# Moving the turns of the S5 tables from ScalarE to VectorE, scans with a constant factor, and more buffers

## The chip, the cores and the metric

The kernel runs on one core of a Trainium2 chip. Its engines are named as in the profile: PE is TensorE (PEld its weight loads), DVE is VectorE, ACT is ScalarE, POOL is GpSimd, SP is SyncE. Each engine works through its own queue in order; engines wait for one another through semaphores. The metric is the device time in microseconds (us), lower is better. The time before is 2409.3 us, the median of three runs (2407.95 to 2409.64).

## The reference

One inference step of a two-layer backbone over 2048 latent tokens and 128 context tokens. The even layer has a gated linear attention branch and an S5 branch, the odd layer attention and a short convolution. Only the S5 branch is touched. It is a diagonal complex recurrence, run forward and backward over 32 groups of 16 channels with 64 complex states each:

```
bu_re = einsum('blgh,gph->blgp', u, bb_re);  bu_im = einsum('blgh,gph->blgp', u, bb_im)
h_t   = lb * h_(t-1) + bu_t            # complex, lb = exp(lam * dt), per state
h_re  = hf_re + flip(hb_re);  h_im = hf_im + flip(hb_im)
y5    = einsum('blgp,ghp->blgh', h_re, c_re) - einsum('blgp,ghp->blgh', h_im, c_im)
z     = gelu(y5 + s5_d * u)
```

The final states of the 128 context tokens are outputs too.

## The kernel before

The program is written with a tile framework that gives out buffers from pools and sets the order of each engine's queue by a timing model of its own, so the order below is that of the built program and not that of the Python lines. Everything is fp32; a large matmul is done as three passes over a high and a low part (`mm3`, lines 100 to 102).

Stages follow each other: input projection to u, v and gates (up to about 275 us); then the S5 core, woven with a dense projection (`qz_pass`, accumulated in the two `psD` banks and evicted by ACT into `fo`, lines 811 to 815); then GLA, GLU, the output projection and the odd layer.

The S5 core (`s5_core`) treats the 16 tokens of a chunk at once, so that a recurrence over 136 chunks (128 latent, 8 context) is left. The complex factor over a chunk is split into a magnitude, `s5_m16`, and a unit rotation. Tables C and S hold the powers of the rotation: column n of a table is the rotation by n. With them the complex recurrence becomes a real one on rotated values. One group goes through three steps:

- `first(g)`: the Toeplitz block `tz` by DMA; every second group the tables of two groups (`tables`, called when g is even); the gate tile `rgo` (line 675), which is the magnitude times a mask of ones that has a zero where the latent and the context sequence meet; and the input weights `e` on POOL.
- `second(g)`: PE transposes u into one of the three tiles `s5U` and e into `winc`, both evicted by ACT; PE multiplies them (line 708, into psW). DVE rotates the product (lines 714 to 717), runs two scans of 138 columns, one for each direction (line 722), and rotates back to H (`rh`, lines 723 to 726).
- `third(g)`: PE adds four products into psW (lines 735 to 738), ACT takes the gelu into `zy` (line 740) and stores it by two DMAs from its own queue, and copies the two final states out of H (line 731).

`weights(g + 5)` on POOL (lines 583 to 585) prepares the output weights `ct`, seven buffers, which line 738 reads last.

A table is built by doubling. ACT copies the first 16 columns, column 128 and the 9 columns of the context from small tables (lines 626 to 628). Then for m = 16, 32 and 64 the m first columns are turned by m: ACT multiplies both parts by the sine (line 637, into `tabw`), and DVE adds or subtracts the part times the cosine (line 641). For two groups and two directions that is 12 instructions on ACT and 24 on DVE, and each m needs the columns of the one before. The tables of two groups have two buffers.

A quad is four groups. The program takes 8 of the dense pass's blocks (24 matmuls each) for every quad.

Of the kernel before, what the change touches and what calls it, by code (L numbers as in the profile page):

```python
# [14 lines left out]
F32 = mybir.dt.float32  # L15
# [4 lines left out]
AF = mybir.ActivationFunctionType  # L20
OP = mybir.AluOpType
# [27 lines left out]
class Kernel:  # L49
# [317 lines left out]
    def s5_setup(self, es):  # L367
# [10 lines left out]
        self.s5_BB = c.tile([128, 2, 64, 17], F32, name="s5B")  # L378
        self.s5_A = [self.s5_AA[:, j] for j in range(2)]
        self.s5_B = [self.s5_BB[:, j] for j in range(2)]  # L380

        self.s5_go = c.tile([128, 2, 138], F32, name="s5go")
        nc.gpsimd.memset(self.s5_go, 1.0)
        nc.gpsimd.memset(self.s5_go[:, 0, 129:130], 0.0)
        nc.gpsimd.memset(self.s5_go[:, 1, 128:129], 0.0)
        self.s5_m16 = c.tile([128, 64], F32, name="s5m16")
        self.s5_h0 = self.load(c, "s5h0", a["s5h0"])
        self.s5_fin = c.tile([128, 2, 32], F32, name="s5fin")
# [1 line left out]
        self.s5_dc = self.load(c, "dcol", a["dcol"])  # L390
        sg = self.load(c, "sgn", a["sgn"])
        self.s5_U = []
        for j in range(3):
            u = c.tile([128, 2, 139], F32, name=f"s5U{j}")
            for z in (0, 129, 138):
                nc.gpsimd.memset(u[:, :, z : z + 1], 0.0)
            self.s5_U.append(u)
# [167 lines left out]
    def s5_core(self, es):  # L565
# [50 lines left out]
        def tables(g0):  # L616

            t = p.tile([128, 2, 2, 2, 138], F32, name="tabs", tag="tabs", bufs=2)
            AA, BB = self.s5_AA, self.s5_BB
            for d in range(2):  # L620
                dg = slice(d * 32 + g0, d * 32 + g0 + 2)

                at = (lambda m, n: slice(m, m + n)) if d == 0 else (lambda m, n: slice(129 - m - n, 129 - m))
                rev = (lambda n: slice(0, n)) if d == 0 else (lambda n: slice(n - 1, None, -1))
                e = 128 if d == 0 else 0
                nc.scalar.copy(t[:, :, d, :, at(0, 16)], BB[:, :, dg, rev(16)].rearrange("p c g n -> p g c n"))
                nc.scalar.copy(t[:, :, d, :, e], AA[:, :, dg, 8].rearrange("p c g -> p g c"))
                nc.scalar.copy(t[:, :, d, :, 129:138], BB[:, :, dg, rev(9)].rearrange("p c g n -> p g c n"))
            four = [(d, gg) for d in range(2) for gg in range(2)]
            for m in (16, 32, 64):  # L630

                turn = lambda j, d, gg: AA[:, j, d * 32 + g0 + gg, m // 16 : m // 16 + 1]
                at = lambda d, a: slice(a, a + m) if d == 0 else slice(129 - m - a, 129 - a)
                ws = []
                for d, gg in four:
                    ws.append(p.tile([128, 2, 64], F32, name="tabw", tag="tabw", bufs=6)[:, :, 0:m])
                    nc.scalar.activation(ws[-1], t[:, gg, d, :, at(d, 0)], AF.Copy, scale=turn(1, d, gg))  # L637
                for (d, gg), w in zip(four, ws):
                    for j, op in ((0, OP.subtract), (1, OP.add)):
                        x = t[:, gg, d, j]  # L640
                        V.scalar_tensor_tensor(x[:, at(d, m)], x[:, at(d, 0)], turn(0, d, gg), w[:, 1 - j], op0=OP.mult, op1=op)  # L641
            return t

        uv = self.u_d[0:NLAT, :].rearrange("(c t) f -> c t f", t=16)
        up = self.u_d[NLAT:NT, :].rearrange("(c t) (g h) -> c g t h", t=16, h=16)
        quad, tabs, es, tzs, Hs, gos = {}, {}, {}, {}, {}, {}

        def first(g):

            q = g // 4  # L650
            if g % 4 == 0:
                uc = p.tile([128, 16, 64], F32, name="uc", tag="uc", bufs=1)
                nc.sync.dma_start(uc, uv[:, :, 64 * q : 64 * q + 64])
                ugp = p.tile([32, 16, 16], F32, name="ugp", tag="ugp", bufs=1)
                for j in range(4):
                    nc.sync.dma_start(ugp[8 * j : 8 * j + 8], up[:, 4 * q + j])
                ug = p.tile([128, 4, 16, 16], F32, name="ug", tag="ug", bufs=2)
                nc.scalar.copy(ug, uc.rearrange("c t (g h) -> c g t h", g=4))

                pt = self.bank("T", (128, 2, 32))  # L660
                for kt in range(2):
                    nc.tensor.transpose(pt[:, kt], ugp[:, 8 * kt : 8 * kt + 8, :], self.ident[0:32, 0:32])
                ut = p.tile([128, 2, 32], F32, name="ugt", tag="ugt", bufs=2)
                nc.scalar.copy(ut, pt)
                quad[q] = ug, ut
            tz = tzs[g] = p.tile([128, 2, 256], F32, name="tz", tag="tz", bufs=2)
            src = self.f_d[g]
            for kt in range(2):
                sa = bass.AP(tensor=src.tensor, offset=src.offset + kt * 128, ap=[[16, 8], [496, 16], [1, 256]])
                nc.sync.dma_start(tz[:, kt, :], sa)  # L670
            if g % 2 == 0:
                tabs[g // 2] = tables(g)
            go = gos[g] = p.tile([128, 2, 138], F32, name="rgo", tag="rgo", bufs=3)
            for d in range(2):
                nc.scalar.activation(go[:, d], self.s5_go[:, d], AF.Copy, scale=self.s5_m16[:, d * 32 + g : d * 32 + g + 1])
            e = es[g] = pw_.tile([128, 2, 16, 16], F32, name="e", tag="e", bufs=2)
            for d in range(2):
                dg = d * 32 + g
                t1 = pw_.tile([128, 16, 16], F32, name="e1", tag="ct1", bufs=2)
                fl = (lambda v: v[:, dg, 15::-1]) if d == 0 else (lambda v: v[:, dg, 0:16])  # L680
                pw = lambda v: fl(v).unsqueeze(2).to_broadcast([128, 16, 16])
                xv = lambda v: v[:, d, g, :].unsqueeze(1).to_broadcast([128, 16, 16])
                G.tensor_tensor(t1, pw(M), xv(self.s5_Y), op=OP.mult)
                G.tensor_tensor(e[:, d], pw(R), xv(self.s5_X), op=OP.mult)
                G.tensor_tensor(e[:, d], e[:, d], t1, op=OP.add)

        def second(g):

            ug, ut = quad[g // 4]
            U = self.s5_U[g % 3]  # L690
            pt = self.bank("T", (128, 2, 128))
            for kt in range(2):
                v = slice(8 * kt, 8 * kt + 8)
# [13 lines left out]
                for kt in range(2):  # L707
                    nc.tensor.matmul(pi[:, d, :], w[:, d, kt, :], U[:, kt, d : d + 138], start=kt == 0, stop=kt == 1)
            C, S = (tabs[g // 2][:, g % 2, :, j] for j in range(2))
            go = gos.pop(g)  # L710
            A_ = p.tile([128, 2, 138], F32, name="ra", tag="ra", bufs=2)
            B_ = p.tile([128, 2, 138], F32, name="rb", tag="rb", bufs=2)
            H = Hs[g] = p.tile([128, 2, 138], F32, name="rh", tag="rh", bufs=2)
# [4 lines left out]
            af = A_.rearrange("p d c -> p (d c)")  # L718
            V.tensor_copy(af[:, 0:267:266], self.s5_h0[:, :, g])
            for d in range(2):  # L720
                sl = slice(0, 138) if d == 0 else slice(137, None, -1)
                V.tensor_tensor_scan(B_[:, d, sl], go[:, d, sl], A_[:, d, sl], 0.0, op0=OP.mult, op1=OP.add)
            V.tensor_tensor(H, B_, C, op=OP.mult)
            V.tensor_tensor(A_[0:64], B_[64:128], S[64:128], op=OP.mult)
            V.tensor_tensor(A_[64:128], B_[0:64], S[0:64], op=OP.mult)
# [1 line left out]

        def third(g):

            U, H, tz, ct = self.s5_U[g % 3], Hs.pop(g), tzs.pop(g), cts.pop(g)  # L730
            nc.scalar.copy(self.s5_fin[:, :, g], H.rearrange("p d c -> p (d c)")[:, 137:268:130])
            py = self.bank("W", (128, 2, 137))
            for kt in range(2):
                o, cs, t0 = py[:, kt], slice(128 * kt, 128 * kt + 128), 8 * kt
                nc.tensor.matmul(o, tz[:, 0, cs], U[:, 0, 1:138], start=True, stop=False)
                nc.tensor.matmul(o, tz[:, 1, cs], U[:, 1, 1:138], start=False, stop=False)
                nc.tensor.matmul(o, ct[:, 0, t0 : t0 + 8, :], H[:, 0, 0:137], start=False, stop=False)
                nc.tensor.matmul(o, ct[:, 1, t0 + 1 : t0 + 9, :], H[:, 1, 1:138], start=False, stop=True)
            zy = late.tile([128, 2, 137], F32, name="zy", tag="zy", bufs=2)
            nc.scalar.activation(zy, py, AF.Gelu_apprx_tanh)  # L740
            for kt in range(2):
                nc.scalar.dma_start(self.z_d[8 * kt : 8 * kt + 8, 16 * g : 16 * g + 16, :], zy[:, kt])

# [66 lines left out]

    def fm_store(self, dst, pc, b, ps, scale=1.0):
        nc = self.nc
        t = self.fo.tile([128, 272], F32, name="fo", tag="fo", bufs=3)
        nc.scalar.activation(t, ps, AF.Copy, scale=scale)  # L814
        nc.scalar.dma_start(dst[b * 128 : (b + 1) * 128, pc * 272 : (pc + 1) * 272], t)

# [10 lines left out]
    def zg_pass(self, hp, blocks):  # L827

        nc = self.nc

        def use(b, pc, ps):
            t = self.fo.tile([128, 272], F32, name="fo", tag="fo", bufs=3)
            nc.scalar.activation(t, ps, AF.Tanh, scale=0.5)
            nc.vector.scalar_tensor_tensor(t, t, 1.0, ps, op0=OP.add, op1=OP.mult)
            nc.gpsimd.dma_start(self.zg_d[b * 128 : (b + 1) * 128, pc * 272 : (pc + 1) * 272], t)

        return self.fm_pass(hp, blocks, use, self.h_d)
# [961 lines left out]
```

## Time and profile before

| What | Value |
|---|---|
| median of three runs | 2409.3 us |
| the profiled execution | 2415.59 us |
| its span, first to last instruction | 2413.7 us |
| mean granted TensorE clock | 0.966 |
| PE, DVE, ACT, POOL busy share of the span | 94%, 69%, 43%, 36% |

The profile is one execution, recorded engine by engine. Its own time is 1.9 us above its span and 6.3 us above the median of the timed runs. "Busy" is the time an engine spends in instructions, "idle before" the time it stood still before them, with the instruction that ended the wait. A busy DVE instruction may hold time in which it waits for memory, so a mean duration is to be compared with the shortest of the same shape.

### The profile page before, as it was taken

How to read it: one execution, taken by the hardware profiler on the slowest of the kernel's cores; microseconds unless marked ns; L12 is line 12 of the kernel's file. 1: busy time of each engine (PE TensorE's matmuls, PEld its weight loads, DVE VectorE, ACT ScalarE, POOL GpSimd, SP SyncE). 2: the span in 40 equal slices, each digit the busy share in tenths (PEclk: the TensorE clock that was granted, in tenths of full speed). 3: DMA queues.
4: the chain of work that ended last, by engine and by line, in shares of the span. 5: the costliest groups of instructions: out<-in, count | busy, mean ns of one | idle time of the engine just before them, and what ended most of it. 6: DMA issues, size and time to landing. Idle time of an engine off the chain costs nothing.

```text
span 2413.7 us, 47276 instructions
## 1 busy us (share of the span) xinstructions
PE 2268.3 (94%) x17473; PEld 2108.3 (87%) x17473; DVE 1659.3 (69%) x3916; ACT 1042.7 (43%) x2533; POOL 867.6 (36%) x1348
## 2 busy tenths in 40 slices
PE   7999887888899987999999999999999997999998
PEld 4988787887897876888888999999999997999998
DVE  4997688888866776888887665565344336676765
ACT  3554644343544453455454432233122115565653
POOL 4127165566522227767674021111101102222221
PEclk9999988999999995999999999999999998999999
DMA  9765853343469873333333642245133223222221
GB/s 322 236 210 181 252 162 99 102 132 110 131 212 310 291 232 100 123 119 123 116 115 102 210 120 80 80 138 147 50 93 102 68 69 100 88 89 88 90 69 58
DMA packets 328040, 332.90 MB, mean 138 GB/s; under 512 B 43969, under 2 KB 274977, under 8 KB 327809
## 3 DMA queue, kind: packets, MB, share of 16 engines
q1 hardware_dynamic: 265312, 238.84, 33.1%
q0 software_dynamic: 14384, 48.65, 5.9%
q10 hardware_dynamic: 48112, 42.38, 5.4%
q8 instruction: 138, 2.26, 0.4%
q14 instruction: 94, 0.76, 0.1%
HBM read 223.57 MB, written 106.22 MB: 137 GB/s over the span
## 4 chain that ended last, share of the span: by engine, by line
PE 57%; DVE 8%; issue 4%; DMA 4%; ACT 2%; POOL 2%; SPq 0%; ACTq 0%; POOLq 0%; DVEq 0%
PE psD L100 7%; PE psW L100 7%; PE psW L101 7%; PE psW L102 7%; PE psD L102 7%; PE psD L101 7%; PE psP L1081 3%; PE psW L1510 2%; PE psW L1463 2%; DVE tabs L641 2%; PE psT L1498 2%; PE psP L1098 1%; PE psP L1096 1%; DMA wst<-in_w_in_o_dram 1%; DMA wst<-h_d 1%
## 5 line engine op out<-in xcount | busy, mean ns | idle before, releaser
L100 PE MATMUL psD<-slot,yT 128*128 128x256 f32 x1088 | 318.2, 293 | 1.9 <-ACT yT L1125 1.9
L102 PE MATMUL psD<-slot,yT 128*128 128x256 f32 x1088 | 314.1, 292 | 0.0
L101 PE MATMUL psD<-slot,yT 128*128 128x256 f32 x1088 | 310.7, 286 | 0.0
L101 PE MATMUL psW<-hq,slot 128*128 128x272 f32 x1024 | 293.0, 287 | 0.0
L102 PE MATMUL psW<-hq,slot 128*128 128x272 f32 x1024 | 292.9, 287 | 0.0
L100 PE MATMUL psW<-hq,slot 128*128 128x272 f32 x1024 | 289.1, 287 | 0.0
L100 PE MATMUL psD<-hq,slot 128*128 128x272 f32 x768 | 235.1, 308 | 46.8 <-ACT fo L814 45.8
L101 PE MATMUL psD<-hq,slot 128*128 128x272 f32 x768 | 230.0, 300 | 0.0
L102 PE MATMUL psD<-hq,slot 128*128 128x272 f32 x768 | 229.5, 300 | 0.0
L100 PEld LDWEIGHTS psD<-slot,yT 128*128 128x128 f32 x1088 | 208.1, 191 | 10.0 <-ACT yT L1125 2.0
L102 PEld LDWEIGHTS psD<-slot,yT 128*128 128x128 f32 x1088 | 205.8, 191 | 4.5 <-issue 2.2
L101 PEld LDWEIGHTS psD<-slot,yT 128*128 128x128 f32 x1088 | 208.1, 191 | 1.8
L100 PEld LDWEIGHTS psD<-hq,slot 128*128 128x128 f32 x768 | 151.8, 199 | 55.2 <-ACT fo L814 48.8
L102 PEld LDWEIGHTS psW<-hq,slot 128*128 128x128 f32 x1024 | 193.1, 189 | 0.0
L101 PEld LDWEIGHTS psW<-hq,slot 128*128 128x128 f32 x1024 | 192.5, 188 | 0.0
L100 PEld LDWEIGHTS psW<-hq,slot 128*128 128x128 f32 x1024 | 190.6, 188 | 0.0
L641 DVE SCALAR_TENSOR_TENSOR tabs<-tabs,s5A,tabw 128x16 f32<-128x16 f32 (+2 forms) x384 | 146.8, 447 | 24.9 <-ACT tabw L637 23.5
L101 PEld LDWEIGHTS psD<-hq,slot 128*128 128x128 f32 x768 | 152.1, 198 | 6.4 <-issue 4.7
L102 PEld LDWEIGHTS psD<-hq,slot 128*128 128x128 f32 x768 | 152.1, 198 | 1.0 <-issue 1.0
L1472 DVE CUSTOM_DVE_ANT_0 sc<-psW,amask,sink 128x512 f32<-128x512 f32 (+1 forms) x128 | 93.6, 732 | 84.7 <-PE psT L1498 76.2
L1007 ACT ACTIVATE arg<-arg 128x512 f32<-128x512 f32 x119 | 75.0, 631 | 143.6 <-POOL arg L1006 140.3
L1475 ACT ACTIVATE sc<-sc,nm 128x512 f32<-128x512 f32 (+1 forms) x128 | 90.9, 710 | 87.9 <-DVE nm L1474 74.8
(376 smaller groups left out, 6543.2 us busy)
## 6 DMA issues: line engine op xcount, KB each, us to landing
wst<-h_d SPq DMA_DIRECT2D x96, 272.0 KB
hq<-hl_d SPq DMA_DIRECT2D x40, 544.0 KB
hl_d<-ht POOLq DMA_DIRECT2D x17, 1024.0 KB, 6.7
wada<-in_w_ada_dram SPq DMA_DIRECT2D x32, 512.0 KB
h_d<-hf SPq DMA_DIRECT2D x17, 512.0 KB
x_d<-x ACTq DMA_DIRECT2D x17, 512.0 KB
h_d<-hf ACTq DMA_DIRECT2D x17, 512.0 KB
wst<-h_d SPq DMA_DIRECT2D x34, 256.0 KB
```

Source lines behind the costliest of these rows:

```text
L100: mm(out, lh, rh, start=start, stop=False)
L101: mm(out, lh, rl, start=False, stop=False)
L102: mm(out, ll, rh, start=False, stop=stop)
L641: V.scalar_tensor_tensor(x[:, at(d, m)], x[:, at(d, 0)], turn(0, d, gg), w[:, 1 - j], op0=OP.mult, op1=op)
L1007: nc.scalar.activation(arg, arg, AF.Exp, scale=0.0625)
L1081: nc.tensor.matmul(pv[:, hh, pr, :], ak[o : o + 64, pr, :], aq[o : o + 64, pr, :], start=True, stop=True)
L1096: nc.tensor.matmul(ot, qh[o : o + 64, 0, pr, :], sf[o : o + 64, pr], start=True, stop=False)
L1463: nc.tensor.matmul(out, r32(qs[:, j, h]), kk, start=j == 0, stop=j == 1)
L1472: V.tensor_tensor_reduce(sv, ps, mask, 1.0, sk[:, h : h + 1], op0=OP.add, op1=OP.max, accum_out=m)
L1475: nc.scalar.activation(sv, src, AF.Exp, bias=nm[:, h : h + 1], accum_out=sm[:, h : h + 1])
L1498: nc.tensor.transpose(pt[:, c, :], t[:, 128 * c : 128 * c + 128], self.ident)
L1510: nc.tensor.matmul(po[kv][:, j % 2], r32(VV[:, b, kv]), r32(t[:, x, :, c, :]), start=c + x == 0, stop=c + x == nb)
```

## The change

The turns by the sine move from ACT to DVE (line 637), so a table's doubling needs no other engine after ACT's first copies. The gate tile and its mask go: a scan takes the magnitude as a constant, one column read again and again, and is split at the border of latent and context, so there are 128 and the scans have 129 and 9 columns in place of 64 of 138. There are four `s5U` tiles in place of three. The copy of the final states is written behind the gelu and kept there by the framework's `keep_in_program_order`. `zy` has three buffers in place of two and `fo` four in place of three.

```
-        self.s5_go = c.tile([128, 2, 138], F32, name="s5go")
-        nc.gpsimd.memset(self.s5_go, 1.0)
...
-        for j in range(3):
+        for j in range(4):
             u = c.tile([128, 2, 139], F32, name=f"s5U{j}")
...
                     ws.append(p.tile([128, 2, 64], F32, name="tabw", tag="tabw", bufs=6)[:, :, 0:m])
-                    nc.scalar.activation(ws[-1], t[:, gg, d, :, at(d, 0)], AF.Copy, scale=turn(1, d, gg))
+                    V.tensor_scalar(ws[-1], t[:, gg, d, :, at(d, 0)], turn(1, d, gg), None, op0=OP.mult)
...
-            go = gos[g] = p.tile([128, 2, 138], F32, name="rgo", tag="rgo", bufs=3)
-            for d in range(2):
-                nc.scalar.activation(go[:, d], self.s5_go[:, d], AF.Copy, scale=self.s5_m16[:, d * 32 + g : d * 32 + g + 1])
...
             for d in range(2):
-                sl = slice(0, 138) if d == 0 else slice(137, None, -1)
-                V.tensor_tensor_scan(B_[:, d, sl], go[:, d, sl], A_[:, d, sl], 0.0, op0=OP.mult, op1=OP.add)
+                m = self.s5_m16[:, d * 32 + g : d * 32 + g + 1]
+                for lo, n in ((0, 129), (129, 9)):
+                    sl = slice(lo, lo + n) if d == 0 else slice(lo + n - 1, lo - 1 if lo else None, -1)
+                    V.tensor_tensor_scan(B_[:, d, sl], m.to_broadcast([128, n]), A_[:, d, sl], 0.0, op0=OP.mult, op1=OP.add)
...
-            nc.scalar.copy(self.s5_fin[:, :, g], H.rearrange("p d c -> p (d c)")[:, 137:268:130])
...
-            zy = late.tile([128, 2, 137], F32, name="zy", tag="zy", bufs=2)
+            zy = late.tile([128, 2, 137], F32, name="zy", tag="zy", bufs=3)
             nc.scalar.activation(zy, py, AF.Gelu_apprx_tanh)
+            self.tc.keep_in_program_order(nc.scalar.copy(self.s5_fin[:, :, g], H.rearrange("p d c -> p (d c)")[:, 137:268:130]))
...
-        t = self.fo.tile([128, 272], F32, name="fo", tag="fo", bufs=3)
+        t = self.fo.tile([128, 272], F32, name="fo", tag="fo", bufs=4)
```

DVE's queue at the tables that stand around an even group, before (`tabs` are the tables, `psW` the product of line 708, `rb` the scanned values):

```order
L641 SCALAR_TENSOR_TENSOR tabs<-tabs,s5A,tabw 128x32 x4
L714 TENSOR_TENSOR ra<-tabs,psW 128x276
L715 TENSOR_TENSOR rb<-tabs,psW 64x276
L716 TENSOR_TENSOR rb<-tabs,psW 64x276
L641 SCALAR_TENSOR_TENSOR tabs<-tabs,s5A,tabw 128x32 x4
L641 SCALAR_TENSOR_TENSOR tabs<-tabs,s5A,tabw 128x64 x4
L717 TENSOR_TENSOR ra<-ra,rb 128x276
L641 SCALAR_TENSOR_TENSOR tabs<-tabs,s5A,tabw 128x64 x4
L719 COPY ra<-s5h_1897 128x2
L722 SCALAR_TENSOR_TENSOR rb<-rgo,ra 128x138 x2
```

The same place in the changed program, whose line numbers are some lines lower (L632 is the turn that was L637, L636 was L641, L705 to L708 were L714 to L717, L715 is the scan):

```order
L636 SCALAR_TENSOR_TENSOR tabs<-tabs,s5A,tabw 128x32 x8
L632 TENSOR_SCALAR tabw<-tabs,s5A 128x128
L705 TENSOR_TENSOR ra<-tabs,psW 128x276
L706 TENSOR_TENSOR rb<-tabs,psW 64x276
L707 TENSOR_TENSOR rb<-tabs,psW 64x276
L632 TENSOR_SCALAR tabw<-tabs,s5A 128x128 x3
L636 SCALAR_TENSOR_TENSOR tabs<-tabs,s5A,tabw 128x64 x2
L708 TENSOR_TENSOR ra<-ra,rb 128x276
L636 SCALAR_TENSOR_TENSOR tabs<-tabs,s5A,tabw 128x64 x6
L710 COPY ra<-s5h_1893 128x2
L715 SCALAR_TENSOR_TENSOR rb<-s5m_1892,ra 128x9 x2
L715 SCALAR_TENSOR_TENSOR rb<-s5m_1892,ra 128x129 x2
```

The turns now stand among the additions that read them, and each scan has become two; the group's own instructions keep their places.

ACT's queue where the tables of the next pair begin, before:

```order
L626 COPY tabs<-s5B 128x2x2x16
L731 COPY s5fin<-rh 128x2
L627 COPY tabs<-s5A 128x2x2
L815 DMA zs_d<-fo 128x272
L704 COPY winc<-psT 128x512
L628 COPY tabs<-s5B 128x2x2x9
L637 ACTIVATE tabw<-tabs,s5A 128x2x16 x2
L675 ACTIVATE rgo<-s5go,s5m_1896 128x138
```

And in the changed program (L621 to L623 are the first copies of the tables, L732 the gelu, L807 the eviction of the dense pass, L687 and L696 those of `s5U` and `winc`):

```order
L732 ACTIVATE zy<-psW 128x274
L733 COPY s5fin<-rh 128x2
L735 DMA z_d<-zy 8x16x137 x2
L807 ACTIVATE fo<-psD 128x272
L621 COPY tabs<-s5B 128x2x2x16
L622 COPY tabs<-s5A 128x2x2
L623 COPY tabs<-s5B 128x2x2x9
L808 DMA zs_d<-fo 128x272
L687 COPY s5U_1910<-psT 128x2x128
L696 COPY winc<-psT 128x512
```

The turns and gate tiles are gone from between the evictions, the final states follow the gelu at once, and the tables' first copies still stand ahead of the evictions of `s5U` and `winc`.

## Rows read from the trace of the kernel before

**Rows 1.** The page, busy time and share of each engine over the span.

```profile
PE 2268.3 (94%) x17473; PEld 2108.3 (87%) x17473; DVE 1659.3 (69%) x3916; ACT 1042.7 (43%) x2533; POOL 867.6 (36%) x1348
```

**Rows 2.** Busy time by stretch: three quads and the core's end; columns named first.

```profile
core 0: us, PE busy (x) PEld busy (x) DVE busy (x) ACT busy (x) POOL busy (x), PEclk, DMA share, GB/s
416.00:467.80 51.80, 43.68 (x330) 41.36 (x330) 42.58 (x95) 21.59 (x76) 32.90 (x49) 0.93 0.38 110
467.80:519.80 52.00, 43.41 (x330) 41.10 (x330) 42.76 (x95) 21.71 (x76) 32.98 (x50) 0.93 0.37 110
519.80:572.90 53.10, 44.58 (x330) 42.25 (x330) 42.51 (x95) 21.71 (x76) 32.82 (x49) 0.90 0.36 107
670.50:705.00 34.50, 33.40 (x271) 32.79 (x270) 24.18 (x56) 11.52 (x32) 3.95 (x6) 1.00 0.55 175
```

**Rows 3.** Waits of DVE, 285 to 700 us: total us, times, longest.

```profile
DVE ra L714 <- PE psW L708: 32.1, 11, 4.8
DVE tabs L641 <- ACT tabw L637: 23.5, 15, 2.1
```

**Rows 4.** Waits of ACT in the same stretch.

```profile
ACT tabw L637 <- DVE tabs L641: 59.8, 67, 4.0
ACT s5fin L731 <- DVE rh L726: 41.3, 28, 4.3
ACT rgo L675 <- DVE rb L722: 25.7, 12, 5.1
```

**Rows 5.** Waits of PE in the same stretch.

```profile
PE psD L100 <- ACT fo L814: 45.8, 13, 5.6
```

**Rows 6.** Groups on DVE, 285 to 700 us: busy us, mean ns | idle before.

```profile
L641 DVE SCALAR_TENSOR_TENSOR tabs<-tabs,s5A,tabw 128x16 f32<-128x16 f32 x128 | 58.6, 524 | 24.4 <-ACT tabw L637 23.5 <-issue 0.9
L641 DVE SCALAR_TENSOR_TENSOR tabs<-tabs,s5A,tabw 128x64 f32<-128x64 f32 x128 | 45.4, 414 | 0.2
L641 DVE SCALAR_TENSOR_TENSOR tabs<-tabs,s5A,tabw 128x32 f32<-128x32 f32 x128 | 44.7, 402 | 0.3
L722 DVE TENSOR_TENSOR_SCAN rb<-rgo,ra 128x138 f32<-128x138 f32 x64 | 35.0, 587 | 1.0
L724 DVE TENSOR_TENSOR ra<-rb,tabs 64x276 f32<-64x276 f32 x32 | 19.9, 623 | 0.4
L725 DVE TENSOR_TENSOR ra<-rb,tabs 64x276 f32<-64x276 f32 x32 | 19.5, 608 | 0.4
L726 DVE TENSOR_TENSOR rh<-rh,ra 128x276 f32<-128x276 f32 x32 | 19.1, 597 | 1.0
L723 DVE TENSOR_TENSOR rh<-rb,tabs 128x276 f32<-128x276 f32 x32 | 18.3, 572 | 1.0
```

**Rows 7.** DVE in order of time, 515 to 575 us: start, us, instructions.

```profile
523.84 0.86 DVE L641 SCALAR_TENSOR_TENSOR tabs<-tabs,s5A,tabw 128x64 f32<-128x64 f32 x4
524.63 0.15 DVE L719 COPY ra<-s5h 128x2 f32<-128x2 f32 x1
524.81 0.78 DVE L722 TENSOR_TENSOR_SCAN rb<-rgo,ra 128x138 f32<-128x138 f32 x2
526.09 0.44 DVE L724 TENSOR_TENSOR ra<-rb,tabs 64x276 f32<-64x276 f32 x1
544.44 4.64 DVE L641 SCALAR_TENSOR_TENSOR tabs<-tabs,s5A,tabw 128x64 f32<-128x64 f32 x8
```

**Rows 8.** POOL in order of time, 515 to 575 us.

```profile
547.13 1.26 POOL L583 TENSOR_TENSOR ct<-s5M,s5CY 128x272 f32<-128x272 f32 x2
559.15 1.40 POOL L584 TENSOR_TENSOR ct<-s5R,s5CX 128x272 f32<-128x272 f32 x2 [9.57 <-PE psW L738]
```

**Rows 9.** POOL's groups, 285 to 700 us: first and last of six.

```profile
L685 POOL TENSOR_TENSOR e<-e,e 128x256 f32<-128x256 f32 x60 | 43.9, 752 | 0.0
L583 POOL TENSOR_TENSOR ct<-s5M,s5CY 128x272 f32<-128x272 f32 x50 | 31.5, 651 | 0.0
```

**Rows 10.** A DVE multiplication by a column, in the setup, 100 to 300 us.

```profile
L416 DVE TENSOR_SCALAR s5M<-q,sgn 128x64 f32<-128x64 f32 x1 | 0.3, 279 | 0.0
```

More of the change, by code (lines that the diff above doesn't have):

```diff
@@ L380, in s5_setup @@
         self.s5_B = [self.s5_BB[:, j] for j in range(2)]
-        self.s5_go = c.tile([128, 2, 138], F32, name="s5go")
-        nc.gpsimd.memset(self.s5_go, 1.0)
-        nc.gpsimd.memset(self.s5_go[:, 0, 129:130], 0.0)
-        nc.gpsimd.memset(self.s5_go[:, 1, 128:129], 0.0)
         self.s5_m16 = c.tile([128, 64], F32, name="s5m16")
@@ L645, in s5_core @@
         up = self.u_d[NLAT:NT, :].rearrange("(c t) (g h) -> c g t h", t=16, h=16)
-        quad, tabs, es, tzs, Hs, gos = {}, {}, {}, {}, {}, {}
+        quad, tabs, es, tzs, Hs = {}, {}, {}, {}, {}
         def first(g):
@@ L689, in second @@
             ug, ut = quad[g // 4]
-            U = self.s5_U[g % 3]
+            U = self.s5_U[g % 4]
             pt = self.bank("T", (128, 2, 128))
@@ L709, in second @@
             C, S = (tabs[g // 2][:, g % 2, :, j] for j in range(2))
-            go = gos.pop(g)
             A_ = p.tile([128, 2, 138], F32, name="ra", tag="ra", bufs=2)
@@ L728, in third @@
         def third(g):
-            U, H, tz, ct = self.s5_U[g % 3], Hs.pop(g), tzs.pop(g), cts.pop(g)
-            nc.scalar.copy(self.s5_fin[:, :, g], H.rearrange("p d c -> p (d c)")[:, 137:268:130])
+            U, H, tz, ct = self.s5_U[g % 4], Hs.pop(g), tzs.pop(g), cts.pop(g)
             py = self.bank("W", (128, 2, 137))
@@ L831, in use @@
         def use(b, pc, ps):
-            t = self.fo.tile([128, 272], F32, name="fo", tag="fo", bufs=3)
+            t = self.fo.tile([128, 272], F32, name="fo", tag="fo", bufs=4)
             nc.scalar.activation(t, ps, AF.Tanh, scale=0.5)
```

## The prediction

> **What bounds the kernel now.** I read the busy shares first. PE is busy 94% of the span [rows 1], so a change can help only where PE stands still. The stretches show one such place, and it is the one that the change touches: in the S5 core a quad of groups takes about 52 us, PE is busy 43 to 45 us of it at a granted clock of 0.90 to 0.93, and DVE 42.5 to 42.8 us [rows 2]. Both have 8 to 10 us to spare in every quad, so neither is the bound by itself: they wait for each other. After 670 us PE is busy 33.4 of 34.5 us at full clock, so there DVE has slack and PE sets the pace [rows 2].
>
> The waits tell how. PE stands 45.8 us before a dense matmul because ACT has not yet evicted `fo` [rows 5]. ACT is late because its queue is held by things that need DVE: 59.8 us before a turn whose columns DVE has not added yet, 41.3 us before the copy of the final states, 25.7 us before a gate tile whose buffer the scan still reads [rows 4]. PE's lateness comes back to DVE, which waits 32.1 us for the product of line 708, and 23.5 us for a turn [rows 3]. That is 55.6 us of waiting on DVE in a stretch of 415 us. The rest of DVE's time is work, and one more thing has to be seen in it: the same instruction has two prices. Four additions of 64 columns take 0.86 us at 523.84, eight of them 4.64 us at 544.44, which is 0.215 and 0.58 each [rows 7]. At the first POOL is idle (its next instructions stand behind waits such as the 9.57 us before 559.15), at the second it runs without a break, two instructions in 1.26 us [rows 8]. So while POOL runs, DVE gets about one instruction in for each of POOL's, whatever its length, and a hit costs 0.58 - 0.215 = 0.365 us.
>
> How many hits there are: the additions are busy 58.6 + 45.4 + 44.7 = 148.7 us, where 384 at 0.215 are 82.6, an excess of 66 us; the scans 35.0 where 64 at 0.39 (0.78 for two) are 25.0, an excess of 10; the four rotations of lines 723 to 726 76.8 where 128 at 0.44 are 56.3, an excess of 20 [rows 6, 7]. Together 96 us, or 265 hits. POOL has 328 instructions in the stretch (six groups of 50 to 60 [rows 9]), so some 63 of them hit nothing today: they fall on DVE's waits or on instructions that read psW.
>
> **The change part by part.** *The waits.* With no turn and no gate tile on ACT, and the final states copied behind a gelu whose input has needed H anyway, nothing in ACT's queue waits for DVE any more but the tables' first copies. The evictions of `fo`, `s5U` and `winc` come when PE has produced them, a fourth `s5U`, a third `zy` and a fourth `fo` keep them from waiting for a buffer, and PE can bring the next product of line 708 before DVE wants it: after a group's H, PE needs a quarter of a quad's 43 us, about 11, to the next product, and DVE has a whole group or a table in hand. So I take the 55.6 us as gone, bounds 44 to 55.6. What stays is the hand-over at the tables' first copies, which stand in ACT's queue behind a gelu and wait for line 725; they run beside line 726, so I leave 3 us of the 23.5 (bounds 0 and half, 11.8). PE's 45.8 us are not counted again: PE will stand as long, now before line 737, waiting for H, because DVE is then what is late.
>
> *The turns.* DVE gets 192 of them. The trace of before has none on DVE in this place. From below, no DVE instruction is shorter than the 0.15 us of the two-column copy [rows 7]: 28.8 us. From above by itself, a multiplication by a column took 0.279 us [rows 10]: 53.6 us. The nearest row is the addition in the same table, which also reads the table with a column as its factor, at 0.215: 41.3 us, and that I take. ACT loses the work, but ACT is busy only 22 of 52 us in a quad [rows 2], so that alone is worth nothing.
>
> *The scans.* Each becomes one of 129 columns, shorter by 9/138 of 0.39 = 0.025 us, and one of 9, at the least 0.15 us. 64 times 0.125 is 8 us; if as many of the short ones meet POOL as additions do today (66/0.365 = 181 of 384, 47%), it is 8 + 64 x 0.47 x 0.365 = 19.
>
> *POOL.* The turns put 12 more instructions into each of 16 table runs, just where POOL works. Since POOL lets one through for each of its own, the new hits are bounded by the 63 of its instructions that hit nothing today: 0 to 23 us. I take half, 12, because the turns and not the psW readers now fill POOL's stretches, while waits of DVE beside an idle POOL become work beside an idle POOL. The Trainium skill, "SBUF — State Buffer", section "SBUF: two separate sides", says that DVE and GpSimd share a port pair as an exclusive lock, held for a whole instruction, and that a DVE instruction of one source in a two-port mode takes it as one with two inputs does; by that rule a turn is hit like an addition, which is the first rival's case. The doubling of the additions' price agrees with it; a full exclusion the trace does not show, for the 42.8 us of DVE and 33.0 of POOL stand in one quad of 52.
>
> *The end.* After 670 us one pair's turns (12 at 0.215) and four groups' short scans (8 at 0.125) lie beside a PE that is the bound: 3.6 us that cost nothing. The buffers of `zy` and `fo`, and the fourth `s5U`, add no instruction but three small memsets on POOL, where the three of the mask go. Later stages have the same instructions.
>
> *Sum.* -55.6 + 3 + 41.3 + 8 + 12 - 3.6 = +5.1 us. On the profiled execution (span 2413.7 us, with 1.9 us around it 2415.6) that is 2420.7; against the median of 2409.3, which lies 6.3 us lower, it is 2414.4 us, and I say 2414. All bounds at once: -55.6 + 28.8 + 8 - 3.6 = -22 and -44 + 11.8 + 53.6 + 19 + 23 = +63 us.
>
> **The rivals.**
> *The turns meet POOL (slower).* Place: the table runs, between line 726 of an odd group and line 714 of the next. If turns and short scans are hit in 47% of the cases, as the additions are, that is 192 x 0.47 x 0.365 = 33 us and 11 more, in place of 12: 2446. For it: twelve additions in a row at the present are all hit where a POOL stretch covers a table's start. Against it: 265 + 90 + 30 hits are more than POOL's 328 instructions. With all 328 hit it is +11 over my sum, 2425. I give it 2435. It decides from my 33 hits on: each further one is loss that can be told.
> *The hand-over stays (slower).* The tables' first copies stand in ACT's queue ahead of the evictions of `s5U` and `winc`. If ACT reaches them early, those evictions wait for line 725, PE gets its product late, and half of the 32.1 us stays: 2430. For it: the order in ACT's queue. Against it: the product is wanted only after the table run.
> *DVE has room (faster).* If turns pass at 0.15 us, one behind another, and POOL's stretches move with PE's earlier line 738 so that no more is hit, it is -55.6 + 3 + 28.8 + 8 - 3.6 = -19.4 us: 2390. For it: the waits of rows 3 are real and all have their cause in ACT. Against it: DVE then works 50 of 52 us in a quad, and any lateness of PE comes on top.
>
> **How the numbers follow.** My own case (2405 to 2424 us, about even) 42%; turns meet POOL 20%; hand-over stays 8%; DVE has room 30%. A measurement of this kernel can tell about 0.2%, or 4.8 us, from no change. Faster by more: the last rival and a little of my own case, 33%. Within: 24%, the lower half of my case. Slower: its upper part, 15%, and the two slower rivals, 43% together. The 80% range goes from just below the faster rival to just above the first slower one, 2388 to 2442.
>
> **What would show it.** Right: DVE's waits before line 714 and in the tables fall under 10 us from 55.6; DVE is busy over 95% of a quad; PE's wait of 45.8 us before the dense matmul is gone and stands before line 737 for H; quads take 50 to 54 us; the turns are busy 50 to 65 us, with the hits. Wrong: PE busy all through a quad with quads under 49 us (the faster rival); the turns busy over 80 us with additions still at 0.4 to 0.5 us (the first); DVE still waiting over 15 us for line 708 (the second). If quads differ little and the time moves by more than 10 us, the cause lies in a later stage, whose order the framework also shifted, and none of this speaks of it.

## The result, and the profile after

The changed kernel takes 2424.0 us (median of 4 runs, 2423.6 to 2424.3) against 2408.7 for the one before (median of 4 as well): a ratio of 1.0063, 95% interval 1.0046 to 1.0081. It is slower, by 15 us, where 2414 was predicted, 5 us slower. The profiled execution has a span of 2421.7 us, and the page's first part is to be read against [rows 1]:

```profile
PE 2257.5 (93%) x17473; PEld 2107.2 (87%) x17473; DVE 1725.2 (71%) x4172; ACT 968.5 (40%) x2277; POOL 862.1 (36%) x1348
```

DVE has 66 us more, ACT 74 less. Three quads and the core's end, with the columns of [rows 2]:

```profile
420.10:470.30 50.20, 43.61 (x341) 41.12 (x339) 49.30 (x120) 12.39 (x44) 33.48 (x50) 0.97 0.40 116
470.30:522.30 52.00, 43.83 (x330) 41.53 (x330) 49.79 (x127) 12.26 (x44) 32.84 (x48) 0.90 0.37 110
522.30:574.10 51.80, 43.62 (x330) 41.25 (x330) 49.97 (x128) 12.16 (x44) 32.58 (x48) 0.90 0.37 110
673.20:704.50 31.30, 30.97 (x250) 30.34 (x249) 24.94 (x73) 8.36 (x21) 3.73 (x6) 1.00 0.59 193
```

A quad is about as long as before, but DVE is now busy 49.30, 49.79 and 49.97 us of it, where it was 42.5 to 42.8. The waits of the changed kernel between 285 and 715 us (total, times, longest) stand against [rows 3], [rows 4] and [rows 5]; line 705 was 714, 632 was 637, 719 was 726, 729 was 737, 807 was 814:

```profile
PE psW L729 <- DVE rh L719: 56.4, 13, 8.4
PE psD L100 <- ACT fo L807: 3.0, 2, 2.1
...
DVE tabw L632 <- ACT tabs L621: 4.0, 4, 1.3
...
DVE ra L705 <- PE psW L700: 1.3, 1, 1.3
...
ACT tabs L621 <- DVE ra L718: 34.8, 10, 10.4
```

DVE's 55.6 us of waiting are 5.3. PE's 45.8 us before the dense matmul are 3.0, and PE stands 56.4 us before line 729 for H instead. And DVE's groups in the same stretch, against [rows 6]:

```profile
L636 DVE SCALAR_TENSOR_TENSOR tabs<-tabs,s5A,tabw 128x16 f32<-128x16 f32 x128 | 54.2, 484 | 0.0
L636 DVE SCALAR_TENSOR_TENSOR tabs<-tabs,s5A,tabw 128x64 f32<-128x64 f32 x128 | 47.8, 436 | 0.2
L636 DVE SCALAR_TENSOR_TENSOR tabs<-tabs,s5A,tabw 128x32 f32<-128x32 f32 x128 | 34.6, 335 | 0.1
L632 DVE TENSOR_SCALAR tabw<-tabs,s5A 128x32 f32<-128x32 f32 x64 | 32.8, 557 | 4.0 <-ACT tabs L621 4.0
L715 DVE TENSOR_TENSOR_SCAN rb<-s5m,ra 128x129 f32<-128x129 f32 x64 | 28.0, 479 | 0.0
L632 DVE TENSOR_SCALAR tabw<-tabs,s5A 128x64 f32<-128x64 f32 x64 | 25.2, 447 | 0.0
...
L632 DVE TENSOR_SCALAR tabw<-tabs,s5A 128x128 f32<-128x128 f32 x64 | 18.8, 339 | 0.2
...
L715 DVE TENSOR_TENSOR_SCAN rb<-s5m,ra 128x9 f32<-128x9 f32 x64 | 11.7, 224 | 0.0
```

The turns are busy 32.8 + 25.2 + 18.8 = 76.8 us, the additions 54.2 + 47.8 + 34.6 = 136.6 (148.7 before). All of DVE's work from 285 to 715 us, before and then changed (the columns are those of [rows 2]):

```profile
285.00:715.00 430.00, 366.97 (x2719) 346.41 (x2718) 346.37 (x789) 194.35 (x643) 231.66 (x334) 0.92 0.47 137
```

```profile
285.00:715.00 430.00, 364.00 (x2737) 344.87 (x2736) 403.44 (x1050) 119.01 (x385) 230.39 (x334) 0.91 0.48 139
```

DVE works 57.1 us more, and PE's work in the stretch is the same within 3 us.

So DVE's waits became work, and no quad is longer. To see where the time is, I cut each execution into stages by the starts and ends of the same lines: the end of phase 1's last matmul (line 345), the core to the last addition of H, from there to the last store of `fo` in the zg pass, the opening of GLA up to the first of its 17 squares of `x` (line 1193 of before), the 17 chunks from first to last of these, and the rest. The before column has two profiles of the same kernel, the second one taken with the experiments. All in us:

```
kernel                  phase 1   core   to zg   GLA opens  17 chunks   rest     span
before, first profile     269.0  430.1   201.0      81.6      373.5   1058.5   2413.7
before, second            269.6  427.3   196.8      80.4      372.7   1056.9   2403.7
changed                   273.5  427.4   196.7      91.2      378.1   1054.8   2421.7
```

The core lost nothing: 427.4 us against 428.7, the mean of the two. GLA, which the diff does not touch, takes 10 us more to open and 5 more for its chunks. Phase 1's 4 us stay unexplained: PE, DVE and ACT have the same instructions in the same order there in both kernels, and the two profiles of before are themselves up to 2.5 us apart within it. Their spans differ by 10 us.

What is late there shows on POOL, in order of time (start, us, and in brackets the idle time before and what ended it). The changed kernel:

```profile
897.11 0.54 POOL L828 DMA_DIRECT2D zg_d<-fo  x1
900.92 0.10 POOL L965 MEMSET two<- 128x2 f32 x1 [3.27 <-DMA zg_d<-fo]
901.07 0.22 POOL L967 MEMSET two<- 64x1 f32 x2
901.57 0.55 POOL L882 DMA_DIRECT2D ys_d<-gzs  x1 [0.27 <-issue]
910.51 0.40 POOL L996 TENSOR_TENSOR arg<-B 128x128 f32<-128x128 f32 x1 [8.40 <-DMA B<-b_d]
```

`two` is a small constant of GLA. Its memset runs at 276 us in both profiles of before; here it waits for the last transfer out of an `fo` buffer, and the first chunk's arguments (`arg`), which began at 832 and 828 us, begin at 910.5, behind the load of their input `B`. Why that load is late shows on SP, which issues it (start, us; the changed kernel):

```profile
900.85 0.34 SPq L80 DMA_DIRECT2D lmask<-in_lmask_dram  x1
...
906.29 0.46 SPq L1014 DMA_DIRECT2D B<-b_d  x1
```

GLA's mask, `lmask`, waits for the same transfer out of `fo` until 900.8 us, and the load of `B` stands behind it in SP's queue. Such a wait is what the framework lays where two tiles share memory at different times. Nothing in the core is in this chain.

### The profile page after: what moved, and what is told of

Same layout as the page of the kernel before. It is cut to its first block, busy times and chain, and to the rows that moved or that the text cites. A ratio compares the mean times of both kernels' runs of the same rounds, so it can differ in the third digit from the quotient of the medians.

```text
span 2421.7 us, 47202 instructions
## 1 busy us (share of the span) xinstructions
PE 2257.5 (93%) x17473; PEld 2107.2 (87%) x17473; DVE 1725.2 (71%) x4172; ACT 968.5 (40%) x2277; POOL 862.1 (36%) x1348
## 4 chain that ended last, share of the span: by engine, by line
PE 59%; DVE 21%; issue 7%; DMA 6%; POOL 3%; ACT 3%; SPq 1%; ACTq 0%; POOLq 0%; DVEq 0%
PE psD L100 7%; PE psW L102 7%; PE psW L101 7%; PE psW L100 7%; PE psD L102 7%; PE psD L101 7%; DVE tabs L636 5%; PE psW L1503 2%; PE psW L1456 2%; DVE tabw L632 2%; PE psP L1074 2%; PE psT L1491 2%; PE psD L345 2%; PE psW L344 1%; DVE rb L715 1%
## 5 line engine op out<-in xcount | busy, mean ns | idle before, releaser
L100 PE MATMUL psD<-hq,slot 128*128 128x272 f32 x768 | 230.3, 302 | 7.2 <-ACT fo L807 3.0
L101 PE MATMUL psD<-hq,slot 128*128 128x272 f32 x768 | 227.0, 297 | 0.0
L102 PE MATMUL psD<-hq,slot 128*128 128x272 f32 x768 | 226.3, 296 | 0.0
L100 PEld LDWEIGHTS psD<-hq,slot 128*128 128x128 f32 x768 | 148.2, 194 | 12.9 <-ACT hq L231 4.0
L102 PEld LDWEIGHTS psD<-hq,slot 128*128 128x128 f32 x768 | 149.1, 194 | 2.5 <-issue 2.5
L101 PEld LDWEIGHTS psD<-hq,slot 128*128 128x128 f32 x768 | 148.6, 194 | 3.1 <-issue 1.2
L636 DVE SCALAR_TENSOR_TENSOR tabs<-tabs,s5A,tabw 128x16 f32<-128x16 f32 (+2 forms) x384 | 136.0, 418 | 0.3
```

Of the source, the lines that this page charges most:

```text
L100: mm(out, lh, rh, start=start, stop=False)
L101: mm(out, lh, rl, start=False, stop=False)
L102: mm(out, ll, rh, start=False, stop=stop)
```

## The experiments

The stages of all kernels are in one table, and each run below is read from it.

```
kernel                                   phase 1   core   to zg   GLA opens  17 chunks   rest
changed, fo 3 (e1)                         268.8  429.4   194.9      83.1      367.5   1055.0
before, fo 4 (e2)                          269.9  431.4   197.8      93.2      378.1   1055.8
before, unused tile (e3)                   269.4  430.6   197.2      89.8      377.7   1055.1
changed, fo 3, turns on ACT (e5)           268.3  401.1   199.4      83.9      379.4   1055.2
changed, fo 3, half the turns on ACT (e6)  268.9  414.8   194.6      82.7      378.2   1055.2
changed, fo 3, a third of POOL (e7)        262.4  351.2   196.9      81.4      374.4   1057.7
before, turns on DVE (e8)                  269.2  450.7   197.1      83.4      372.4   1055.5
before, copy pinned (e9)                   270.1  422.5   194.1      82.4      374.5   1055.2
turns on ACT, fo 2 (e10)                   267.4  399.6   202.6      83.1      367.1   1055.7
turns on ACT, last 4 tables DVE (e11)      272.3  409.4   195.9      79.7      373.9   1057.4
```

**e1, e2, e3: is it the fourth `fo` buffer?** e1 is the changed kernel with, in both places where `fo` is given out,

```diff
-tag="fo", bufs=4
+tag="fo", bufs=3
```

> The changed kernel with three fo buffers in place of four, all else as changed. Theory A (the step of the prediction: the loss is DVE's new work in the core): the core stays as it is, PE waits a little more for fo, and the time stays at 2422 to 2428 us. Theory B (the fourth fo buffer moves the addresses of the GLA tiles onto tiles that are live until the end of the zg pass, so that the two-column memset of gla_setup and the first chunk's arguments start at 901 to 917 us where they started at 276 to 846, and the GLA stage takes 12 us more until it is in step): the memset goes back to about 280 us, the first chunks come as before, and the time is 2409 to 2415 us.

Measured: 2400.5 us, ratio to before 0.9957 (0.9945 to 0.9970). By the medians that is 23 us under the changed kernel, and 9 faster than the end of B's range: besides the opening, which is back at 83 us, the chunks take 367.5 us. The core is what it was. The memset and the first argument in e1, then the two loads on SP:

```profile
275.47 0.10 POOL L965 MEMSET two<- 128x2 f32 x1 [7.17 <-PE psW L344]
...
850.62 0.40 POOL L996 TENSOR_TENSOR arg<-B 128x128 f32<-128x128 f32 x1 [2.19 <-DMA B<-b_d]
```

```profile
828.52 0.34 SPq L80 DMA_DIRECT2D lmask<-in_lmask_dram  x1
...
841.80 0.83 SPq L1014 DMA_DIRECT2D B<-b_d  x1
```

e2 is the kernel before with `bufs=4`.

> The kernel before with four fo buffers in place of three, nothing else. Theory A: the evictions wait less, part of PE's 45.8 us before the dense matmul goes, 2400 to 2410 us. Theory B: the core gains little or nothing, the arguments of the first GLA chunk come after 900 us, and the time is 2416 to 2422 us.

Measured: 2426.4 us, 1.0056 (1.0044 to 1.0069). That is B, 4 us beyond its range. One buffer more makes the old kernel as slow as the changed one. It does not even help where it was meant to; PE's wait in the core of e2 stands against [rows 5]:

```profile
PE psD L100 <- ACT fo L814: 46.2, 13, 5.7
```

45.8 us with three buffers, 46.2 with four: PE waits for ACT to read its bank, and one more place to write to changes nothing.

e3 leaves the three buffers and puts an idle tile behind them:

```diff
 self.fo = self.pool(eA, "fill", 1, side="right")
+self.pad = self.fo.tile([128, 272], F32, name="pad")
```

> The kernel before with one tile more in the pool of fo, of the size of one fo buffer, that nothing writes or reads. Theory A: no instruction is added, 2408 to 2410 us. Theory B: the addresses move as with a fourth buffer, so the time is that of the kernel before with four buffers, 2416 to 2422 us.

Measured: 2423.1 us, 1.0050 (1.0037 to 1.0064). That is B, 1 us beyond its range. No instruction is added or touched, and POOL reads as in the changed kernel:

```profile
900.50 0.10 POOL L972 MEMSET two<- 128x2 f32 x1 [3.31 <-DMA zg_d<-fo]
```

So it is the memory that the pool takes, not its use. That `two` and `lmask` come to lie on `fo` is inferred from this wait; the addresses were not read.

**e4: the kernel before again.**

> The kernel before once more, for a second profile. Its profiled execution took 2415.6 us where the median is 2409. Both theories: about 2408 to 2410 us; if the 6.3 us lay in the first 285 us, this profile reaches the first quad 5 us later or earlier than 311.2 us; the GLA chunks take 24 to 25 us each, none 35.

Measured: 2409.8 us, 1.0002 (0.9990 to 1.0014); its profile is the second line of the first table. The 6.3 us by which the first profile was off were not in the first 285 us: here the core is 2.8 us shorter, the stage after it 4.2. A profile of this kernel can be off by some us in a stage, and terms below that size cannot be read from one.

**e5, e6: what do the turns cost?** With three `fo` buffers, e5 puts the turns back on ACT and keeps the rest of the change:

```diff
-V.tensor_scalar(ws[-1], t[:, gg, d, :, at(d, 0)], turn(1, d, gg), None, op0=OP.mult)
+nc.scalar.activation(ws[-1], t[:, gg, d, :, at(d, 0)], AF.Copy, scale=turn(1, d, gg))
```

> The changed kernel with three fo buffers and the turns back on ACT; the split scans, the pinned final-state copy, four U and three zy stay. The core is counted from the last matmul of line 345 (phase 1, about 269 us) to the last H: 430.1 and 427.3 us in the two profiles of before, 429.4 with three fo buffers and the turns on DVE. Theory A (DVE is the bound, so that the turns' 79 us on DVE lengthen the core, less the 23.5 us of waits that they remove): the core falls to 375 to 395 us, the time to 2350 to 2370. Theory B (the waits come back with the turns, since ACT's queue waits for DVE at each turn and holds PE's evictions meanwhile): DVE's waits are over 40 us again, the core is 418 to 430 us, the time 2390 to 2405.

Measured: 2388.3 us, 0.9905 (0.9890 to 0.9920); core 401.1 us. It lies between the theories: against e1 the core falls by 28 us, not by the 35 to 55 of A, and DVE's waits do not come back as B says. The time falls by 12 us only, mostly because GLA's chunks take 379.4 us in place of 367.5. DVE's and then PE's waits in the core of e5:

```profile
DVE ra L705 <- PE psW L700: 9.7, 8, 4.0
DVE tabs L636 <- ACT tabw L632: 7.4, 14, 1.9
```

```profile
PE psD L100 <- ACT fo L807: 22.1, 6, 4.9
PE psW L700 <- ACT winc L696: 8.4, 3, 4.0
PE psW L729 <- DVE rh L719: 5.5, 3, 3.4
```

17 us of DVE's waits are left of 55.6, with the turns on ACT. So 38.5 us of that wait go without moving the turns, with the pinned copy, the gate tiles and the buffers. And the turns on DVE cost 28 us of the core, for waits that were nearly gone without them.

e6, also with three `fo` buffers, leaves only half of them on DVE (`if gg:` ACT, else DVE).

> As the changed kernel with three fo buffers, but of the four turns of a step the two of the odd group are on ACT and the two of the even one on DVE, first to be done. Theory A: DVE loses 39 us of work and waits little, since ACT turns two while DVE turns two and adds: core 390 to 400 us, time 2362 to 2375. Theory B: ACT's queue waits for DVE as in the kernel before, and what DVE loses in work it waits: core 415 to 430, time 2388 to 2402.

Measured: 2398.9 us, 0.9950 (0.9938 to 0.9963); core 414.8, in the middle between 401.1 and 429.4. A's 390 to 400 is missed, B's 415 to 430 is at its edge, and the time is in B's range. But DVE waits 5.1 us for the product and 0.6 before the additions, so B's reason, that what DVE loses in work it waits, is not borne out: half the turns cost half the price.

**e7: what does POOL do to DVE?** e7 is e1 with two thirds of POOL's work in the core left out: of the three operations that make each half of `ct` and `e` (two products and their sum) one product is left, so the S5 values are others. For `ct`:

```diff
-G.tensor_tensor(t1, pw(M), cv(self.s5_CY), op=OP.mult)
 G.tensor_tensor(ct[:, d], pw(R), cv(self.s5_CX), op=OP.mult)
-G.tensor_tensor(ct[:, d], ct[:, d], t1, op=OP.add)
```

> The changed kernel with three fo buffers, with two thirds of POOL's products in the core left out: of the three operations that make each half of ct and of e (two products and their sum) only the first product stays, so the values of S5 are others. Theory A (a DVE instruction that meets a POOL instruction costs 0.58 us in place of 0.215): the turns fall from 79 to 50 us busy or less, the additions from 136 to about 100, DVE's work by 90 to 110 us in all, and the core until PE bounds it, to 345 to 370 us; time 2320 to 2345. Theory B (a turn and an addition cost 0.4 to 0.5 us by themselves on these strided tables): turns 70 us or more, additions over 125, core 415 or more, time 2388 or more.

Measured: 2321.9 us, 0.9630 (0.9614 to 0.9646), core 351.2 in place of e1's 429.4: A, with the additions at 76.4 us, lower still than its 100. Its additions, turns and one rotation:

```profile
L633 DVE SCALAR_TENSOR_TENSOR tabs<-tabs,s5A,tabw 128x64 f32<-128x64 f32 x128 | 30.7, 303 | 0.0
...
L633 DVE SCALAR_TENSOR_TENSOR tabs<-tabs,s5A,tabw 128x32 f32<-128x32 f32 x128 | 24.5, 256 | 0.0
L633 DVE SCALAR_TENSOR_TENSOR tabs<-tabs,s5A,tabw 128x16 f32<-128x16 f32 x120 | 21.2, 238 | 0.0
L629 DVE TENSOR_SCALAR tabw<-tabs,s5A 128x128 f32<-128x128 f32 x64 | 20.3, 366 | 0.3
L710 DVE TENSOR_TENSOR rh<-rb,tabs 128x276 f32<-128x276 f32 x32 | 16.2, 505 | 2.0
...
L629 DVE TENSOR_SCALAR tabw<-tabs,s5A 128x64 f32<-128x64 f32 x62 | 12.9, 259 | 0.0
L629 DVE TENSOR_SCALAR tabw<-tabs,s5A 128x32 f32<-128x32 f32 x60 | 12.1, 246 | 0.1
```

The smallest form of a turn takes 246 ns where it took 557 in the changed kernel, that of an addition 238 for 484. The turns are 45.3 us (186 of the 192 are in the stretch) in place of 76.8. A quad of e7:

```profile
422.50:461.70 39.20, 39.20 (x325) 37.69 (x324) 34.76 (x127) 12.56 (x46) 10.71 (x16) 1.00 0.50 145
```

PE is busy through the whole of it, and at full clock.

**e8, e9: one part alone.** e8 is the kernel before with the turns on DVE.

> The kernel before with the turns on DVE and nothing else of the change. Theory A (the sum of the prediction): DVE gains 79 us of work less 12 us of cheaper additions and loses 23.5 us of waits before the additions and about half of the 32.1 before line 714, since the copies of the final states and the gate tiles still hold ACT's queue: +25 to +30 us, core about 456, time 2432 to 2440. Theory B (the turns alone hold ACT's queue, and with them all 55.6 us go): core 428 to 440 us, time 2405 to 2420.

Measured: 2428.3 us, 1.0074 (1.0061 to 1.0087), core 450.7, 22 us above before: between the theories, nearer to A, a little under its 25 to 30. ACT's queue is held no less, now by the gate tiles, against 25.7 us in [rows 4], and most of DVE's wait before line 714 is still there, against 32.1 in [rows 3]:

```profile
ACT rgo L675 <- DVE rb L722: 112.4, 19, 11.3
...
DVE ra L714 <- PE psW L708: 23.2, 7, 5.6
```

e9 is the kernel before with nothing but the copy of the final states pinned behind the gelu.

> The kernel before with the copy of the final states behind the gelu and pinned there, nothing else. Theory A (the copy, 41.3 us of ACT's waiting, is what held ACT's queue; the rest of the 27 us that the core gains with the turns on ACT comes from the gate tiles and buffers): DVE's wait before line 714 falls to 15 us or less, the core from 428.7 (mean of two profiles) to 410 to 418 us. Theory B (the gate tiles and turns hold the queue as much): wait over 25 us, core 425 to 432. The time, whose GLA stage is in another order here, is less told: A 2392 to 2404, B 2405 to 2418.

Measured: 2403.6 us, 0.9975 (0.9966 to 0.9985), core 422.5: 6 us less, short of A's 410 to 418 though the time is in A's range. DVE's wait before line 714 is 25.8 us, over B's mark. The copy was not the main thing that held the queue; the other 21 us up to e5 come from the gate tiles with their scans, `s5U` and `zy` together, which were not taken apart.

**e10, e11: does the laid-out order set GLA's time?** Both have the turns on ACT: e10 with two `fo` buffers, e11 with three and the turns of the last tables on DVE. An order here is that of PE's queue in the GLA stage.

> The turns on ACT as in the run with three fo buffers (core 401.1 us, 2388 us), but with two fo buffers. PE's order in the GLA stage is then, row for row, that of the changed kernel with three fo buffers, whose first six chunks went by in 141.7 us and whose seventeen in 367.5, where the run with turns on ACT took 153.3 and 379.4. Theory A (the order that the framework lays out for the GLA stage decides those 12 us, not what happened in the core): GLA 367 to 369 us, core 401 to 408 if two fo buffers make PE wait a little, time 2376 to 2384. Theory B (the GLA stage takes longer because it starts earlier against its transfers): GLA 377 to 381 again, time 2388 or more.

Measured: 2380.7 us, 0.9880 (0.9865 to 0.9895): A, and the fastest that leaves out no work, 43 us under the changed kernel. The chunks take 367.1 us as in e1, whose order it has, with the core of e5. Two `fo` buffers cost the core nothing (399.6 and 401.1 us), and PE waits for `fo` there as with three, 22.1 us above:

```profile
PE psD L100 <- ACT fo L807: 24.0, 8, 4.9
```

> The turns on ACT, but those of the last two of sixteen tables on DVE; three fo buffers. PE's order in the GLA stage is then nearly that of the kernel before (373 us for the seventeen chunks in two profiles). Theory A: the core costs 0 to 4 us more than with all turns on ACT, since two tables are an eighth of the 28 us that the turns cost, and they stand where PE begins to be the bound: 401 to 405 us; GLA 372 to 374, time 2380 to 2386. Theory B (GLA's length does not follow the order): GLA 379, time 2388 to 2392.

Measured: 2386.9 us, 0.9911 (0.9896 to 0.9925). GLA follows its order again, 373.9 us (A). The core is 409.4 us, 8 more than e5 and beyond A. But A's share was counted wrongly: the edit (`if g0 >= 24:`) takes in the tables of groups 24 to 31, which are four of the sixteen, and the trace has 48 of the 192 turns on DVE. That is a quarter, and a quarter of 28 is 7 us. So here too the turns cost about in proportion to their number. PE and DVE are both near full at the core's end there:

```profile
620.00:682.00 62.00, 59.38 (x461) 57.83 (x461) 57.50 (x162) 17.51 (x59) 19.86 (x31) 0.95 0.59 182
```

Which of the two holds the other there is open. The profile is of a run 3.6 us above the median of e11's four.

What the slower order does in the chunks shows in one place. In the changed kernel PE is not full between 1050 and 1100 us (columns as in [rows 2]), where before it was:

```profile
1050.00:1100.00 50.00, 44.71 (x346) 38.08 (x345) 41.48 (x100) 21.73 (x53) 31.83 (x58) 0.90 0.34 102
```

```profile
1050.00:1100.00 50.00, 50.00 (x413) 43.55 (x413) 42.76 (x102) 25.01 (x62) 35.04 (x64) 1.00 0.37 118
```

The first row is of the changed kernel, the second of the one before. ACT waits there (1040 to 1100 us, the changed kernel), in the middle of GLA's first chunks, for a product of PE before an exponential of a later chunk:

```profile
ACT hq L1028 <- PE psP L1091: 15.5, 3, 7.8
```

e2 and e3 have such a stretch at the same place, e5 and e6 between 1000 and 1050 us: PE is busy 46.0 to 46.4 us of 50 in each, and their chunks take 377.7 to 379.4 us. e8, whose chunks take 372.4, has none.

e5 and e6 have nearly the same order as the changed kernel (of PE's last 11850 instructions, 513 and 173 stand in another place; in the kernel before 1320 do) and the same 378 to 379 us, with the constant `two` set early. So GLA's order and its late opening are two effects: the opening costs 9 us (89.8 to 93.2 against 79.7 to 83.9), the order 5 us more or 6 less than before's. What in the core decides between the orders is open.

## Why the prediction was right in sign, and why not by its own sum

*The waits* (-55.6, of which 3 stay): right. 55.6 became 5.3, 2.3 us more than the 3 left for the hand-over.

*The turns* (41.3) *and POOL* (12): 53.3 was predicted, 76.8 were busy. A turn that seldom meets POOL costs 0.24 us (45.3 us for 186 in e7), not 0.215, and it is hit as often as an addition. That is the first rival, "the turns meet POOL", as far as the turns go. But it did not cost its price. As argued against it, other instructions were hit less: the additions fell by 12.1 us, the rotations of [rows 6] from 76.8 to 74.2. DVE's busy time from 285 to 715 us went up by 57.1; the terms of the sum give 41.3 + 8 + 12 = 61.3. The mark "50 to 65 us" for the turns was wrong, and that for the rival (over 80 with additions still at 0.4 to 0.5) nearly met, though the core cost nothing: I should have set marks on DVE's whole busy time, not on one group.

*The scans* (8): 28.0 + 11.7 us for 35.0, 4.7.

*The end* (-3.6): not told apart by any run. In e11 the turns of the last four tables cost 8 us where their share of 28 is 7, so none of them looks free; but a profile can be off by some us.

*The core's sum* was +5.1; the core measured -1.3 (427.4 against 428.7), and +0.7 in e1. That DVE's waits are traded for work, nearly one for one, was right. e1 and e5 split it as the sum does: the turns with POOL and the hand-over, less their 23.5 us of waits, are 41.3 + 12 + 3 - 23.5 = +32.8, and e1 against e5 gives +28.3; the rest, -32.1 + 8 - 3.6 = -27.7, is -27.6 in e5 against before. The parts do not add up so in every order: put into the kernel before by themselves, the turns cost 22.0 us (e8), and the rest then gains 21.3 (450.7 to 429.4).

*The step that failed* is the sentence "Later stages have the same instructions", with the buffers costed at nothing but three memsets. The instructions are the same, and they start later and in another order. The zero for the fourth `fo` buffer is the mis-sized term: it costs 12 to 15 us in the kernel before (e3, e2), about the whole difference of the result, and 23 in the changed one (e1). That the time came out slower, within the range, is owed to it and not to DVE: the sign was right by luck. Without that buffer the same change is 10 us faster than before (e1), with the core at +0.7 us and GLA's chunks 5.6 shorter, by an order that the sum did not see either. The last sentence of the prediction named this case and gave it no price.

*The rivals*: "the hand-over stays" is refuted by DVE's 1.3 us before line 705. "DVE has room" fell with the price of a turn.

*The rule on the shared port pair*, which the Trainium skill ("SBUF — State Buffer", section "SBUF: two separate sides") gives for whole instructions: e7 bears out that a turn of one source is hit as an addition is. From e1 to e7 a turn falls from 0.41 to 0.24 us, an addition from 0.35 to 0.20. Its full exclusion no run shows. That both engines are busy most of one quad, the prediction's reason, does not speak against it, for busy time holds waiting. What speaks against it is that POOL's products of line 683 in the kernel before take 617 ns with DVE idle (median of 7) and 622 with DVE busy all through (39), while DVE gets about one instruction through in the time of each.

## What to carry to other kernels

A tile more in a pool is an edit of every stage that later uses that memory: look in the new order for instructions of untouched stages that have moved, above all small constants and first loads, and price them by what starts behind them. Before work is moved to a busy engine in order to free a queue, take out of that queue what else waits for the same engine; here that took 38.5 of 55.6 us of waiting, and moving the turns on top of it cost 28 us of the core (e5, e1). When the bound moves but the time doesn't, cut both executions into stages and check that the untouched ones are as long as they were.

## What the runs showed of the chip that I had not expected

What DVE pays for POOL is more than the 0.365 us that I took for a hit: with 110 POOL instructions in the core (e7) where e1 has 328, DVE's busy time in the core, counted without overlaps, falls from 408.9 us to 301.9, which is 0.49 us for each that is gone. When the turns leave DVE, others take longer in their place: the four rotations, 74.2 us in the changed kernel, are 84.0 in e5 (22.2 + 22.0 + 20.9 + 18.9).

In the core PE's busy time is shorter where it waits less. The 330 matmuls of a quad are busy 43.6 to 43.8 us at a granted clock of 0.90 in the changed kernel, 42.4 to 42.6 at 0.93 to 0.96 in e5; in the quad of e7 above, where PE does not wait, 325 take 39.2 at 1.00. The floor of a quad is thus near 40 us, not the 43.4 to 44.6 of [rows 2].

In GLA, with PE full at a granted clock of 1.00 in both, the order of the same matmuls is worth 1.5% (372.7 us for the chunks in before's second profile, 367.5 in e1). The 64-row products, 1000 to 1290 us, in these two:

```profile
L1081 PE MATMUL psP<-arg 64*128 64x128 f32 x672 | 63.0, 297 | 0.0
```

```profile
L1074 PE MATMUL psP<-arg 64*128 64x128 f32 x680 | 58.1, 294 | 0.0
```

The record of each is as long, but in e1 they overlap more: 680 fill 58.1 us where 672 filled 63.0, and from the start of one to the start of PE's next instruction it is 78 ns in place of 85 in the mean. What in the order does that is open.
